# Recurrent mixer of a two-layer encoder: GpSimd's casts, splits, squares and sums placed on ScalarE and VectorE

## The chip, the core and the metric

One core of a Trainium2 chip runs the whole forward pass of a small encoder: TensorE (PE in the profile) for matrix products, VectorE (DVE), ScalarE (ACT), GpSimd (POOL) and SyncE (SP), which issues most loads. The metric is the device time of one execution in microseconds; lower is better.

## The reference

Two layers over 512 tokens of width 1024. Each layer is a mixer, a layer norm, a mixture of 16 experts and a second layer norm. The first layer mixes by attention, the second by a gated linear recurrence, and only that one is touched:

```python
def rg_lru(xc, w_a, b_a, w_x, b_x, lam, reverse):
    r = sigmoid(block_diag_linear(xc, w_a, b_a))
    i = sigmoid(block_diag_linear(xc, w_x, b_x))
    log_a = LRU_C * r * log_sigmoid(lam)
    a = exp(log_a)
    b = sqrt(-expm1(2.0 * log_a)) * (i * xc)
    _, h = associative_scan(combine, (a, b), reverse=reverse, axis=1)
    return h

def mixer_rglru(x, ...):
    gate, xr = split(x @ w_in, 2, axis=-1)
    xc = conv_b + sum(xp[:, k:k + seq] * conv_w[k] for k in range(4))
    h = rg_lru(xc, forward) + rg_lru(xc, backward)
    y = h * gelu(gate, approximate=True)
    return y @ w_out
```

All of it is in float32.

## The kernel before, in words

**Operands in two parts.** TensorE works here on rounded operands (type fp32r). Each float32 matrix is therefore split into a rounded part, the high half, and the rest, the low half, and a product is three matmuls: high by high, high by low and low by high. The split of a weight chunk of 128x1024 is two instructions in `plain`: a cast, which writes `wh`, and a subtraction, which writes `wl`. Nearly everywhere ScalarE casts (line 133) and VectorE subtracts (line 134). For the recurrent mixer two switches of `plain`, `hp` and `lp`, place the cast on GpSimd (line 131) and the subtraction on GpSimd as well. The string `CONV_X` says for each half chunk of the x projection which of these holds (b: cast on GpSimd; c: subtraction on GpSimd; so they alternate), and `MIXED2` says it for the gate projection: both casts, and the second subtraction.

**Loads.** `Stream` and `Items` hold the weights in the order of use. A chunk is 1 MB (or 512 KB of gate weights) and lands in one of two buffers (`raw`); its load is issued by SyncE when the chunk two before it has been split. `hl` has four pairs of high and low tiles. In the mixer the chunks come in this order: x0, x1, x2, w0, x3, w1, g0, w2, g1, w3, g2, g3; x and g are chunks of the two halves of the input projection (two half chunks each), w are gate weights. In the names of the trace half chunks 217 and 218 belong to x2, 219 to w0, 220 and 221 to x3, 222 to w1, 223 and 224 to g0, 225 to w2, 226 and 227 to g1, 228 to w3, 229 and 230 to g2, 231 and 232 to g3; from 233 on they are the output projection's.

**The mixer, `mixer1`.** The channels are worked on in four chunks of 256 (two blocks `f` of 128), with the 512 tokens along the free side. For each chunk: `proj("x")` fills two PSUM tiles; `conv` makes the convolution of four taps, one on ScalarE (line 1071) and three on VectorE (line 1074), and splits the result (lines 1077 and 1078); `gates` makes, for each block and both directions, two gate products (lines 1107 to 1109) into PSUM, two gate tanh (line 1113), the exponential `a` (line 1115), a further tanh (line 1116), the product `i` (line 1117), the square `u` of `a`, on GpSimd (line 1119), and the product of line 1122. `scan` takes the square root of `u` for the whole chunk (line 1126), multiplies (line 1129), makes four scans on VectorE, two directions by two blocks (line 1132), and adds both directions into `yall`, on GpSimd (line 1133). `gelu` works on the gate projection of the chunk: square (line 1085), a multiply and add of two constants (line 1086), the product with x (line 1087), tanh (line 1088), and two products (lines 1089 and 1091). `split` makes the two parts of `yall` (lines 1137 and 1138) for the output projection `out_proj` (lines 918 to 920), which uses the same four PSUM banks as the projections.

**What sets the order.** Each engine takes its instructions in one fixed order. A scheduler of the framework has arranged that order ahead of time from the program; the change thus moves more than the lines it names. Across engines, tiles are guarded by semaphores: a buffer is written again only when its readers are done. The loop of `mixer1` runs one stage late: while chunk c is projected, the gates and scans of the chunk two before it are worked on.

```python
        for k, c2 in (("x", 2), ("x", 3), ("g", 0), ("g", 1)):
            g = c2 - 2 if k == "x" else c2 + 2
            proj(k, c2, 0)
            gates(g, 0)
            proj(k, c2, 1)
            gates(g, 1)
            if k == "x":
                conv(c2)
            scan(g)
            if k == "g":
                gelu(c2)
```

ScalarE holds one table of functions at a time; where the next function isn't in it, an ACT_TABLE_LOAD stands in its order. In the mixer the square root needs a table other than exp and tanh.

Of the kernel before, what the change touches and what calls it, by code (L numbers as in the profile page):

```python
# [20 lines left out]
D = 1024  # L21
# [6 lines left out]
FC = DE // P  # L28
CAP = 96
OV = 13  # L30
CONV_X = "bcbcbcbc"
TAIL = ("a0 m0 a1 m1 v0 v1 h0 f0 h1 f1 a2 m2 a3 m3 v2 v3 h2 f2 h3 f3",
        "a0 m0 a1 m1 v0 a2 m2 v1 k0 f0 a3 m3 v2 h1 f1 v3 h2 f2 h3 f3")
FPOS = (0, 1, 2, 4, 5, 6, 7, 8, 10, 13)
# [67 lines left out]


def layout(I):
    """The inputs as the kernel loads them: slices, copies and permutations of what came in, and constants."""
    c = host_consts()
    a = {n: np.ascontiguousarray(I[n]) for n in _INS}
    rows = lambda x, n: np.broadcast_to(np.asarray(x).reshape(1, n), (P, n))
# [16 lines left out]
    return a  # L125


def plain(a, w, hp=False, lp=False):
    def conv(nc, r, h, l):
        if hp:  # L130
            nc.gpsimd.tensor_scalar(h[:, :w], r[:, a:a + w], 1.0, 1.0, op0=ALU.mult, op1=ALU.mult)
        else:
            nc.scalar.copy(h[:, :w], r[:, a:a + w])  # L133
        (nc.gpsimd if lp else nc.vector).tensor_tensor(l[:, :w], r[:, a:a + w], h[:, :w].bitcast(F32), op=ALU.subtract)  # L134
    return conv


PLAIN2 = (plain(0, HALF), plain(HALF, HALF))
MIXED2 = (plain(0, HALF, True), plain(HALF, HALF, True, True))


class Stream:
# [56 lines left out]
class K:  # L199
# [667 lines left out]
    def mix1_items(self, it):  # L867
        I, nc = self.I, self.nc

        self.first_ins = []  # L870

        def ld_in(c0):
            def load(t):
                ins = nc.sync.dma_start(t.rearrange("p (a b) -> p a b", a=KC),
                                        I["l1_w_in"][:, c0:c0 + 256].rearrange("(a p) b -> p a b", p=P)).ins
                if len(self.first_ins) < 2:
                    self.first_ins.append(ins)
            return load

        def ld_g(c):  # L880
            def load(t):
                nc.sync.dma_start(t[:, :HALF], I["gates"][c])
            return load

        mix = dict(a=(False, False), b=(True, False), c=(False, True), d=(True, True))
        x = lambda c: it.add(("x", c), ld_in(D + 256 * c),
                             tuple(plain(i * HALF, HALF, *mix[CONV_X[2 * c + i]]) for i in range(2)))
        g = lambda c: it.add(("g", c), ld_in(256 * c), MIXED2)
        w = lambda c: it.add(("w", c), ld_g(c), PLAIN2[:1])
        for f, c in ((x, 0), (x, 1), (x, 2), (w, 0), (x, 3), (w, 1), (g, 0), (w, 2), (g, 1), (w, 3), (g, 2), (g, 3)):  # L890
            f(c)
        self.out_items(it, 1)
# [159 lines left out]
    def mixer1(self, st, xH, xL):  # L1052
# [28 lines left out]
        def gelu(c2):  # L1081
            for f in range(2):
                x = B["g", c2][f]
                q = wp.tile([P, S], F32, name=f"ge{c2}{f}", tag="ge", bufs=2)
                A.activation(q, x, AF.Square)
                V.tensor_scalar(q, q, G1 * G2, G1, op0=ALU.mult, op1=ALU.add)
                V.tensor_tensor(q, q, x, op=ALU.mult)
                A.activation(q, q, AF.Tanh)
                V.scalar_tensor_tensor(q, q, 1.0, x, op0=ALU.add, op1=ALU.mult)  # L1089
                c = 2 * c2 + f  # L1090
                V.tensor_tensor(yall[:, c], q, yall[:, c], op=ALU.mult)

        def gates(c2, f):
# [22 lines left out]
                A.activation(r, r, AF.Tanh, bias=cm, scale=cm)  # L1116
                V.scalar_tensor_tensor(ii[:, k], ii[:, k], 1.0, xc[:, f], op0=ALU.add, op1=ALU.mult)
            sl = slice(2 * f, 2 * f + 2)
            nc.gpsimd.tensor_tensor(u[:, sl], a[:, sl], a[:, sl], op=ALU.mult)
            for d in range(2):  # L1120
                k = 2 * f + d
                V.scalar_tensor_tensor(u[:, k], u[:, k], 1.0, tr[d], op0=ALU.add, op1=ALU.mult)
# [1 line left out]
        def scan(c2):  # L1124
            a, ii, u = R[c2]
            A.activation(u, u, AF.Sqrt, scale=1.0 / 16.0)
            for f in range(2):
                sl = slice(2 * f, 2 * f + 2)
                V.tensor_tensor(ii[:, sl], ii[:, sl], u[:, sl], op=ALU.mult)
                for d, o in ((0, slice(None)), (1, slice(None, None, -1))):  # L1130
                    k = 2 * f + d
                    V.tensor_tensor_scan(u[:, k, o], a[:, k, o], ii[:, k, o], 0.0, op0=ALU.mult, op1=ALU.add)
                nc.gpsimd.tensor_tensor(yall[:, 2 * c2 + f], u[:, 2 * f], u[:, 2 * f + 1], op=ALU.add)

        def split(c2):
            for c in (2 * c2, 2 * c2 + 1):
# [584 lines left out]
```

## Time and profile before

| what | value |
|---|---|
| median of 3 runs | 1189.37 us (1189.37 to 1190.99) |
| profiled execution, first to last instruction (span) | 1188.6 us |
| that span beside the median | 0.8 us below it; a separate time of that execution is not listed |
| TensorE matmuls busy | 1056.6 us, 89% |
| VectorE busy | 953.0 us, 80% |
| ScalarE busy | 768.1 us, 65% |
| GpSimd busy | 318.2 us, 27% |
| mean granted TensorE clock | 0.937 |

Busy shares are means over stages that differ: the recurrent mixer takes some 180 of the 1188.6 us, from the end of the first layer at about 595 to the start of the output projection at about 763. What a stage is limited by is read from a window on it, and what an instruction costs from its own line or from the timeline. A mean above the shortest of the same shape says that some of a group's instructions took longer than their work.

### The profile page before, as it was taken

To read this page: it belongs to the slowest core of one execution; us is meant where nothing else is said; L and a number is where in the kernel's file an instruction comes from. 1 tells how busy PE (TensorE), PEld (TensorE's weight loads), DVE (VectorE), ACT (ScalarE), POOL (GpSimd) and SP (SyncE) were. 2 spreads that over 40 slices of the span, in tenths; PEclk is the share of its full clock that TensorE was granted. 3 is DMA by queue.
4 is the path that set the end of the run, shared out by engine and by line. 5 is a ranking of instruction groups with operands and counts; after the bars stand their busy time and mean duration, and the time that the engine had idled before them with its cause. 6 is when DMAs were issued, how large, how long until landed. Compare 5 with 4: busy or idle time off the path is not lost. (4 is left out here: it accounts for less than half of the span.)

```text
span 1188.6 us, 15070 instructions
## 1 busy us (share of the span) xinstructions
PE 1056.6 (89%) x5042; PEld 783.3 (66%) x5042; DVE 953.0 (80%) x1487; ACT 768.1 (65%) x1114; POOL 318.2 (27%) x278
## 2 busy tenths in 40 slices
PE   8999889986999999989789768797799999999892
PEld 6677677874777777756478546586577777776651
DVE  5685878367999999967767999947899998996785
ACT  5455778225788788757526665533578888876762
POOL 1112555125131121111234536203422211210122
PEclk9897999996999999989979969798799999999996
DMA  8180010877999999988713112295799999996983
GB/s 288 54 260 21 2 36 18 335 263 263 324 348 371 360 365 355 345 295 300 188 55 106 35 54 72 87 365 206 269 335 336 380 374 367 387 332 204 335 268 108
DMA packets 132693, 281.25 MB, mean 237 GB/s; under 512 B 8872, under 2 KB 32584, under 8 KB 132480
## 3 DMA queue, kind: packets, MB, share of 16 engines
q1 hardware_dynamic: 121344, 245.20, 56.8%
q0 software_dynamic: 10928, 33.93, 11.9%
q10 hardware_dynamic: 336, 1.08, 0.2%
q8 instruction: 42, 0.69, 0.2%
q14 instruction: 43, 0.35, 0.1%
HBM read 261.41 MB, written 23.74 MB: 240 GB/s over the span
## 5 line engine op out<-in xcount | busy, mean ns | idle before, releaser
L134 DVE TENSOR_TENSOR wl<-rr,wh 128x1024 fp32r<-128x1024 f32 x180 | 212.2, 1218 | 20.9 <-ACT wh L133 20.1
L133 ACT CAST wh<-rr 128x1024 fp32r<-128x1024 f32 x180 | 180.2, 1049 | 39.6 <-PE p L587 34.1
L134 DVE TENSOR_TENSOR wl<-rf,wh 128x1024 fp32r<-128x1024 f32 x104 | 123.8, 1219 | 17.5 <-ACT wh L133 17.3
L133 ACT CAST wh<-rf 128x1024 fp32r<-128x1024 f32 x104 | 105.2, 1048 | 43.4 <-PE p L587 15.1
L134 DVE TENSOR_TENSOR wl<-raw,wh 128x1024 fp32r<-128x1024 f32 (+1 forms) x97 | 116.1, 1225 | 20.2 <-ACT wh L133 11.6
L133 ACT CAST wh<-raw 128x1024 fp32r<-128x1024 f32 (+1 forms) x93 | 92.8, 1031 | 25.5 <-PE p L587 6.0
L636 POOL DMA_INDIRECT ybuf<-y,dst x30 | 57.2, 1907 | 185.7 <-ACT y L635 175.4
L625 PE MATMUL py<-wh,hh 128*96 128x512 f32 x256 | 102.9, 410 | 3.0 <-ACT y L635 1.8
L626 PE MATMUL py<-wl,hh 128*96 128x512 f32 x256 | 102.8, 402 | 1.6 <-DVE wl L134 1.6
L553 POOL DMA_INDIRECT xg<-hbuf,idx x32 | 41.0, 1280 | 236.1 <-PE xt L566 213.2
L583 PE MATMUL p<-wh,xh 128*96 128x512 f32 x256 | 102.8, 401 | 1.4 <-ACT xh L567 1.4
L627 PE MATMUL py<-wh,hl 128*96 128x512 f32 x256 | 102.6, 404 | 0.9 <-DVE hl L605 0.9
L586 PE MATMUL p<-wl,xh 128*96 128x512 f32 x256 | 101.4, 396 | 0.0
L584 PE MATMUL p<-wl,xh 128*96 128x512 f32 x256 | 101.4, 396 | 0.0
L585 PE MATMUL p<-wh,xh 128*96 128x512 f32 x256 | 101.1, 395 | 0.3
L588 PE MATMUL p<-wh,xl 128*96 128x512 f32 x256 | 101.1, 395 | 0.0
L587 PE MATMUL p<-wh,xl 128*96 128x512 f32 x256 | 100.7, 393 | 0.0
L134 DVE TENSOR_TENSOR wl<-rx,wh 128x1024 fp32r<-128x1024 f32 x56 | 66.1, 1219 | 7.6 <-ACT wh L133 7.6
L133 ACT CAST wh<-rx 128x1024 fp32r<-128x1024 f32 x56 | 56.2, 1050 | 9.9 <-PE p L587 7.6
L625 PEld LDWEIGHTS py<-wh,hh 128*96 128x96 f32 x256 | 42.1, 166 | 25.0 <-issue 4.9
L918 PE MATMUL pom<-wh,x 128*128 128x512 f32 x128 | 52.2, 408 | 4.4 <-DVE ge L1089 4.4
L627 PEld LDWEIGHTS py<-wh,hl 128*96 128x96 f32 x256 | 42.5, 166 | 19.8 <-DVE hl L605 1.8
(410 smaller groups left out, 2600.2 us busy)
## 6 DMA issues: line engine op xcount, KB each, us to landing
rr<-l_w SPq DMA_DIRECT2D x124, 512.0 KB, 11.2
rf<-l_w SPq DMA_DIRECT2D x68, 512.0 KB, 13.0
rr<-l_w SPq DMA_DIRECT2D x28, 1024.0 KB, 13.6
rx<-l_w SPq DMA_DIRECT2D x36, 512.0 KB, 10.6
raw<-l_w SPq DMA_DIRECT2D x36, 512.0 KB, 12.9
rf<-l_w SPq DMA_DIRECT2D x15, 1024.0 KB, 13.0
raw<-l_w SPq DMA_DIRECT2D x13, 1024.0 KB, 6.5
raw<-l_w_in SPq DMA_DIRECT2D x11, 1024.0 KB, 5.5
```

The source lines that it names most:

```text
L133: nc.scalar.copy(h[:, :w], r[:, a:a + w])
L134: (nc.gpsimd if lp else nc.vector).tensor_tensor(l[:, :w], r[:, a:a + w], h[:, :w].bitcast(F32), op=ALU.subtract)
L583: nc.tensor.matmul(p1, H[:, kc], w1h[:, sl], start=f, stop=False)
L584: nc.tensor.matmul(p1, H[:, kc], w1l[:, sl], start=False, stop=False)
L585: nc.tensor.matmul(p3, H[:, kc], w3h[:, sl], start=f, stop=False)
L586: nc.tensor.matmul(p3, H[:, kc], w3l[:, sl], start=False, stop=False)
L587: nc.tensor.matmul(p1, L[:, kc], w1h[:, sl], start=False, stop=e)
L588: self.last_mm = nc.tensor.matmul(p3, L[:, kc], w3h[:, sl], start=False, stop=e).ins
L625: nc.tensor.matmul(py[n], H[:, c], a, start=c == 0, stop=False)
L626: nc.tensor.matmul(py[n], H[:, c], b, start=False, stop=False)
L627: nc.tensor.matmul(py[n], L[:, c], a, start=False, stop=c == FC - 1)
L636: nc.gpsimd.indirect_dma_start(out=self.ybuf[l], out_offset=bass.IndirectOffsetOnAxis(ap=dst, axis=0), in_=y, in_offset=None, bounds_check ...
```

## The change

The weights of the mixer are split as everywhere else: cast on ScalarE, subtraction on VectorE. The square of `a` is a Square on ScalarE. The two sums into `yall` become one on VectorE over both blocks. In `gelu` the multiply and add and the product become one instruction, (q + 1/G2) times x, and the constants go into the scale of the tanh. Nothing else is changed; line numbers of the changed kernel are some 3 to 8 lower.

```diff
-CONV_X = "bcbcbcbc"
...
-def plain(a, w, hp=False, lp=False):
+def plain(a, w):
     def conv(nc, r, h, l):
-        if hp:
-            nc.gpsimd.tensor_scalar(h[:, :w], r[:, a:a + w], 1.0, 1.0, op0=ALU.mult, op1=ALU.mult)
-        else:
-            nc.scalar.copy(h[:, :w], r[:, a:a + w])
-        (nc.gpsimd if lp else nc.vector).tensor_tensor(l[:, :w], r[:, a:a + w], h[:, :w].bitcast(F32), op=ALU.subtract)
+        nc.scalar.copy(h[:, :w], r[:, a:a + w])
+        nc.vector.tensor_tensor(l[:, :w], r[:, a:a + w], h[:, :w].bitcast(F32), op=ALU.subtract)
     return conv
...
-MIXED2 = (plain(0, HALF, True), plain(HALF, HALF, True, True))
...
-        mix = dict(a=(False, False), b=(True, False), c=(False, True), d=(True, True))
-        x = lambda c: it.add(("x", c), ld_in(D + 256 * c),
-                             tuple(plain(i * HALF, HALF, *mix[CONV_X[2 * c + i]]) for i in range(2)))
-        g = lambda c: it.add(("g", c), ld_in(256 * c), MIXED2)
+        x = lambda c: it.add(("x", c), ld_in(D + 256 * c))
+        g = lambda c: it.add(("g", c), ld_in(256 * c))
...
                 A.activation(q, x, AF.Square)
-                V.tensor_scalar(q, q, G1 * G2, G1, op0=ALU.mult, op1=ALU.add)
-                V.tensor_tensor(q, q, x, op=ALU.mult)
-                A.activation(q, q, AF.Tanh)
+                V.scalar_tensor_tensor(q, q, 1.0 / G2, x, op0=ALU.add, op1=ALU.mult)
+                A.activation(q, q, AF.Tanh, scale=G1 * G2)
...
-            nc.gpsimd.tensor_tensor(u[:, sl], a[:, sl], a[:, sl], op=ALU.mult)
+            A.activation(u[:, sl], a[:, sl], AF.Square)
...
-                nc.gpsimd.tensor_tensor(yall[:, 2 * c2 + f], u[:, 2 * f], u[:, 2 * f + 1], op=ALU.add)
+            u4 = u.rearrange("p (f d) s -> p f d s", f=2)
+            V.tensor_tensor(yall[:, 2 * c2:2 * c2 + 2], u4[:, :, 0], u4[:, :, 1], op=ALU.add)
```

The order on ScalarE at the end of the gates of the first chunk, up to its square root (`u0` holds the squares, `a0` the exponentials, `xc2` the third chunk's convolution, `wh222` a weight's high half), before:

```order
L1116 ACTIVATE tr10_6651<-tr10_6651,cl_1194 128x512
L1113 ACTIVATE i0_6584<-pg13_6667,hb_1197 128x512
L1115 ACTIVATE a0_6583<-tr11_6665,cl_1194 128x512
L1071 ACTIVATE xc2_6678<-ppx20_6551,call_75 128x512
L1116 ACTIVATE tr11_6665<-tr11_6665,cl_1194 128x512
L1071 ACTIVATE xc2_6678<-ppx21_6552,call_75 128x512
L1126 ACT_TABLE_LOAD
L1126 ACTIVATE u0_6585<-u0_6585 128x2048
L1113 ACT_TABLE_LOAD
```

and of the change:

```order
L1107 ACTIVATE a0_6583<-tr11_6665,cl_1194 128x512
L129 CAST wh222_6707<-raw112_6705 128x1024
L1108 ACTIVATE tr11_6665<-tr11_6665,cl_1194 128x512
L1111 ACTIVATE u0_6585<-a0_6583 128x1024
L1064 ACTIVATE xc2_6678<-ppx20_6551,call_75 128x512
L1064 ACTIVATE xc2_6678<-ppx21_6552,call_75 128x512
L1105 ACTIVATE tr20_6742<-pg20_6738,hb_1197 128x512
L1118 ACT_TABLE_LOAD
L1118 ACTIVATE u0_6585<-u0_6585 128x2048
L1105 ACT_TABLE_LOAD
L1105 ACTIVATE i1_6736<-pg21_6744,hb_1197 128x512
```

The square of `a0` (line 1111) and the cast of `wh222` now stand between the last exponential and the root; the cast stood earlier before, and the square was not on this engine.

The order on VectorE behind the gates of the second chunk (`wl225` is the low half of the third chunk's gate weights; `i1` and `u1` belong to the second chunk; `xc3` is the last convolution), before:

```order
L1122 SCALAR_TENSOR_TENSOR u1_6738<-u1_6738,tr20_6743 128x512
L1122 SCALAR_TENSOR_TENSOR u1_6738<-u1_6738,tr21_6757 128x512
L1117 SCALAR_TENSOR_TENSOR i1_6737<-i1_6737,xc1_6538 128x512 x2
L134 TENSOR_TENSOR wl225_6862<-raw114_6859,wh225_6861 128x1024
L1122 SCALAR_TENSOR_TENSOR u1_6738<-u1_6738,tr30_6804 128x512
L1122 SCALAR_TENSOR_TENSOR u1_6738<-u1_6738,tr31_6818 128x512
L1074 SCALAR_TENSOR_TENSOR xc3_6831<-ppx30_6700,call_75,xc3_6831 128x510
```

and of the change:

```order
L1121 TENSOR_TENSOR i1_6736<-i1_6736,u1_6737 128x1024 x2
L1071 TENSOR_TENSOR xcL3_6840<-xc3_6830,xcH3_6839 128x1024
L1124 SCALAR_TENSOR_TENSOR u1_6737<-a1_6735,i1_6736 128x512 x4
L130 TENSOR_TENSOR wl225_6860<-raw114_6857,wh225_6859 128x1024
L1126 TENSOR_TENSOR yall_6302<-u1_6737 128x1024
L130 TENSOR_TENSOR wl226_6924<-raw115_6921,wh226_6923 128x1024
L1079 SCALAR_TENSOR_TENSOR ge00_6990<-ge00_6990,ppg00_6851 128x512
```

`wl225` stood ahead of the last convolution and of the second chunk's scans; it stands behind the four scans now, and the sum into `yall` (line 1126) and the low halves of the next gate projection follow it.

The order on VectorE from the last chunk's products and scans on (`u3`, `i3`; `wl231` and `wl232` are the low halves of the last gate projection's weights; `ge11` and `ge20` are gelu tiles), before:

```order
L1129 TENSOR_TENSOR i3_7044<-i3_7044,u3_7045 128x1024 x2
L1132 SCALAR_TENSOR_TENSOR u3_7045<-a3_7043,i3_7044 128x512 x4
L1086 TENSOR_SCALAR ge20_7225<-ge20_7225 128x512
L1086 TENSOR_SCALAR ge21_7232<-ge21_7232 128x512
L1087 TENSOR_TENSOR ge20_7225<-ge20_7225,ppg20_7161 128x512
L1087 TENSOR_TENSOR ge21_7232<-ge21_7232,ppg21_7162 128x512
L134 TENSOR_TENSOR wl233_7244<-raw119_7241,wh233_7243 128x1024
L134 TENSOR_TENSOR wl234_7272<-raw119_7241,wh234_7271 128x1024
```

and of the change:

```order
L1121 TENSOR_TENSOR i3_7039<-i3_7039,u3_7040 128x1024 x2
L1124 SCALAR_TENSOR_TENSOR u3_7040<-a3_7038,i3_7039 128x512 x4
L1081 SCALAR_TENSOR_TENSOR ge11_7147<-ge11_7147,ppg11_7003 128x512
L1126 TENSOR_TENSOR yall_6302<-u3_7040 128x1024
L1083 TENSOR_TENSOR yall_6302<-ge11_7147,yall_6302 128x512
L130 TENSOR_TENSOR wl231_7162<-raw118_7159,wh231_7161 128x1024
L130 TENSOR_TENSOR wl232_7190<-raw118_7159,wh232_7189 128x1024
L1079 SCALAR_TENSOR_TENSOR ge20_7217<-ge20_7217,ppg20_7153 128x512
L1079 SCALAR_TENSOR_TENSOR ge21_7223<-ge21_7223,ppg21_7154 128x512
L130 TENSOR_TENSOR wl233_7234<-raw119_7231,wh233_7233 128x1024
```

The low halves of the last projection's weights stand behind the last scans now; before, `wl231` stood further up, ahead of the last chunk's products, and `wl232` was GpSimd's.

## Rows read from the trace of the kernel before

**Rows 1.** Windows: busy us and instruction counts per engine, then clock, DMA share, GB/s.

```profile
760.00:770.00 10.00, 5.72 (x14) 4.11 (x15) 10.00 (x17) 6.22 (x10) 0.00 (x0) 0.66 0.42 152
...
624.90:775.85 150.95, 117.18 (x485) 92.21 (x484) 140.57 (x138) 94.00 (x124) 63.76 (x35) 0.89 0.22 73
```

**Rows 2.** VectorE's groups, 624.8 to 775.85: busy us, mean ns | idle before.

```profile
L1132 DVE TENSOR_TENSOR_SCAN u<-a,i 128x512 f32<-128x512 f32 x16 | 22.6, 1467 | 0.0
L1122 DVE SCALAR_TENSOR_TENSOR u<-u,tr 128x512 f32<-128x512 f32 x16 | 21.5, 1382 | 3.8 <-POOL u L1119 3.8
L1117 DVE SCALAR_TENSOR_TENSOR i<-i,xc 128x512 f32<-128x512 f32 x16 | 20.4, 1295 | 2.9 <-ACT i L1113 2.9
...
L1086 DVE TENSOR_SCALAR ge<-ge 128x512 f32<-128x512 f32 x8 | 7.8, 985 | 0.0
...
L1078 DVE TENSOR_TENSOR xcL<-xc,xcH 128x1024 fp32r<-128x1024 f32 x4 | 4.8, 1212 | 0.4 <-ACT xcH L1077 0.4
```

**Rows 3.** Single lines of VectorE: shortest, median and longest in ns.

```profile
L1117 DVE SCALAR_TENSOR_TENSOR i<-i,xc x16: 662/1459/2379, 640.2 to 741.4; 128x512 f32<-128x512 f32 x16
L1122 DVE SCALAR_TENSOR_TENSOR u<-u,tr x16: 677/690/2897, 647.8 to 743.2; 128x512 f32<-128x512 f32 x16
L1074 DVE SCALAR_TENSOR_TENSOR xc<-ppx,call,xc x24: 731/740/752, 627.2 to 687.5; 128x511 f32<-128x511 f32 x16, 128x510 f32<-128x510 f32 x8
```

**Rows 4.** Timeline of VectorE: start us, us, then line and operation.

```profile
652.72 2.38 DVE L1117 SCALAR_TENSOR_TENSOR i<-i,xc 128x512 f32<-128x512 f32 x1
```

**Rows 5.** Timeline of GpSimd at the same time.

```profile
652.07 2.48 POOL L1119 TENSOR_TENSOR u<-a 128x1024 f32<-128x1024 f32 x1 [0.95 <-ACT a L1115]
```

**Rows 6.** GpSimd's groups, 624 to 777.

```profile
L1119 POOL TENSOR_TENSOR u<-a 128x1024 f32<-128x1024 f32 x8 | 18.8, 2350 | 5.4 <-ACT a L1115 5.4
L134 POOL TENSOR_TENSOR wl<-raw,wh 128x1024 fp32r<-128x1024 f32 x6 | 16.0, 2667 | 5.3 <-ACT wh L133 5.0
L1133 POOL TENSOR_TENSOR yall<-u 128x512 f32<-128x512 f32 x8 | 14.2, 1773 | 45.6 <-DVE u L1132 45.6
L131 POOL TENSOR_SCALAR wh<-raw 128x1024 fp32r<-128x1024 f32 x10 | 13.2, 1328 | 28.4 <-PE ppx L1044 13.8 <-DVE ge L1089 7.2 <-DVE xcL L1078 5.7
```

**Rows 7.** Timeline of ScalarE: two casts, and four instructions in line.

```profile
591.54 1.97 ACT L133 CAST wh<-raw 128x1024 fp32r<-128x1024 f32 x2
...
697.84 0.68 ACT L1113 ACTIVATE i<-pg,hb 128x512 f32<-128x512 f32 x1
698.41 0.82 ACT L1115 ACTIVATE a<-tr,cl 128x512 f32<-128x512 f32 x1
699.11 0.59 ACT L1085 ACTIVATE ge<-ppg 128x512 f32<-128x512 f32 x1
699.59 0.82 ACT L1116 ACTIVATE tr<-tr,cl 128x512 f32<-128x512 f32 x1
```

**Rows 8.** Timeline of ScalarE: the four square roots, and a table load.

```profile
661.04 1.92 ACT L1126 ACTIVATE u<-u 128x2048 f32<-128x2048 f32 x1
...
684.69 1.28 ACT L1126 ACT_TABLE_LOAD   x1
685.99 1.91 ACT L1126 ACTIVATE u<-u 128x2048 f32<-128x2048 f32 x1
...
712.54 1.92 ACT L1126 ACTIVATE u<-u 128x2048 f32<-128x2048 f32 x1
...
745.23 1.91 ACT L1126 ACTIVATE u<-u 128x2048 f32<-128x2048 f32 x1
```

**Rows 9.** Timeline of TensorE: last gate projection, then output projection.

```profile
744.61 0.77 PE L1042 MATMUL ppg<-x,wh 128*128 128x512 f32 x1 [6.36 <-DVE ge L1089]
...
762.72 0.50 PE L918 MATMUL pom<-wh,x 128*128 128x512 f32 x1 [4.44 <-DVE ge L1089]
765.12 0.79 PE L920 MATMUL pom<-wh,x 128*128 128x512 f32 x1 [1.56 <-DVE x L1138]
```

**Rows 10.** DMA issues by line: count, KB, median us from issue to landing.

```profile
raw<-l_w_in SPq DMA_DIRECT2D x11, 1024.0 KB, 5.5
```

## The prediction

> **What bounds the kernel now.** I read the stretches first, then each engine's lines, then the timelines of the stretch that the change touches. The recurrent mixer's core lies at 624.9 to 775.85 us: there VectorE is busy for 140.57 of 150.95 us, TensorE for 117.18 at a mean granted clock of 0.89, ScalarE for 94.00 and GpSimd for 63.76, with the DMA engines at 0.22 [rows 1]. VectorE leaves 10.4 us unused, so it sets the pace, and TensorE is starved by it.
>
> A good part of VectorE's time is not work. The products of line 1117 and line 1122 take 1295 and 1382 ns in the mean [rows 2], but 662 and 677 ns at best and 2379 and 2897 at worst [rows 3]. Line 1074, of the same length but with one operand in PSUM, stays within 731 to 752 ns throughout [rows 3]. The timeline shows what the slow ones have in common: one product started at 652.72 and took 2.38 us, to 655.1 [rows 4]; GpSimd ran its square from 652.07 to 654.55 [rows 5]. So a VectorE instruction whose operands are all in SBUF stands still while GpSimd works there. The excess is 16 x (1.295 - 0.662) = 10.1 us and 16 x (1.382 - 0.677) = 11.3 us, 21.4 together; scans and other lines show some more, which I leave as margin.
>
> For the whole of the moved work the Trainium skill ("SBUF — State Buffer", "Who interferes with whom") gives more: the ports that VectorE and GpSimd share are an exclusive lock, held for a whole instruction, and the loser blocks fully. By that alone up to GpSimd's 18.8 + 16.0 + 14.2 + 13.2 = 62.2 us [rows 6] could come back; the rows show about a third, since GpSimd often runs when VectorE waits or reads PSUM. The measured 21.4 goes into the sum.
>
> **The change part by part.** *Off GpSimd:* 32 instructions of this stretch, 62.2 us [rows 6]. The excess of 21.4 goes with them, if nothing else takes their place; what stays on GpSimd here are two memsets and a few DMA issues.
>
> *Onto VectorE:* six low splits and four joined sums of 128x1024 elements. The split of line 1078 has the same shape, 4.8/4 = 1.2 us [rows 2], so 10 x 1.2 = 12.0. The sums read with a stride; twice a 128x512 product at its best (1.32) is the other bound, 1.2 more in all. *Off VectorE:* eight instructions of line 1086, 7.8 us with their own excess [rows 2]; the product that replaces line 1087 is of line 1117's kind and length and costs the same. VectorE alone: -21.4 + 12.0 - 7.8 = -17.2 us, if it waits no longer than now.
>
> *Onto ScalarE:* ten casts and eight squares of 128x1024 elements. Two casts take 1.97 us [rows 7], 0.98 each; the squares have the same length and count alike: 18 x 0.98 = 17.6 us on an engine with 57 us free in this stretch. So the ScalarE queue has to be followed. The points to follow it by are the four square roots, at 661.04, 685.99, 712.54 and 745.23 [rows 8]: 84.2 us from first to last. Prices in line come from successive starts: gate tanh 0.57, exp (and the second tanh, and the convolution's first term) 0.70, gelu square 0.48 [rows 7]; root 1.92, table load 1.28 [rows 8]. The order of the changed kernel has, from root to root:
> 1. first to second: root, two loads, 7 x 0.57, 10 x 0.70, six casts or squares: 1.9 + 2.6 + 4.0 + 7.0 + 5.9 = 21.4;
> 2. second to third: root, two loads, 10 x 0.57, 8 x 0.70, 2 x 0.48, six: 22.6;
> 3. third to fourth: root, two loads, 9 x 0.57, 8 x 0.70, 2 x 0.48, four: 20.1.
>
> In the second, the gate weights' low split (wl225) now stands behind the four scans on VectorE. Behind the root VectorE has two products, a split, four scans and wl225, eight steps of 1.2 = 9.6 us, while ScalarE runs dry after three casts, two squares and a load, 5.2: it stands 9.6 - 5.2 = 4.4 us, as the gates' matmuls need that split. So 64.1 + 4.4 = 68.5 in place of 84.2: **-15.7**. Ahead of the first root I take a quarter of the excess, 5.4, less a quarter of the added VectorE work, 3.0, plus 1.5 for a square on the chain that falls from 2.48 [rows 5] to 0.98: **-3.9**. Handovers between engines take an instruction's length rather than the spacing in line, about 0.1 (0.67 against 0.57), some 24 times: **+2.4**. The fourth root comes 17.2 earlier, at 728.0.
>
> The end is TensorE's. The last gate projection needs wl231, which VectorE reaches after two products, four scans, a short product, the sum and another short product: 1.9 + 10.8 behind the root's start, at 740.7 with wl231 itself. Its 48 matmuls took from 744.61 to 758.28, where the 4.44 of idleness begins [rows 9]; the same 13.7 brings them to 754.4. The output projection, which started at 762.72 [rows 9], can follow at once, as by then two PSUM pairs and the first splits are ready: -8.3. It also loses its wait of 1.56 at 765.12 [rows 9], and it no longer enters after 4.44 us of idleness: the granted clock was 0.66 at 760 to 770 [rows 1], partly 1.2 and partly 2.4 GHz, so 0.34 x 10 = 3.4. Sum: -8.3 - 1.6 - 3.4 = **-13.3 us**. From there TensorE's work and the weight loads follow as before: the loads wait for buffers that these same splits free, so they move along with them.
>
> The profiled span is 1188.6, the median 1189.37, 0.8 above it; 1188.6 - 13.3 + 0.8 = **1176.1 us**. Before 624.9 the moved casts and splits cost nothing that I count: two splits land in VectorE's wait for the last expert; if that cover failed they would cost 2.4, about what two collisions there give back.
>
> **Rivals.**
> *More comes back.* Scans and the layer norm ahead of this stretch lose collisions too, and TensorE stays at its high clock. VectorE without a wait would need 140.57 - 17.2 = 123.4 us of 150.95, so 27.6 is the most; three quarters of the 14.3 beyond my sum give 1165. For it: the scans' 1467 ns spread [rows 2] is not in my sum. Against: three engines now share the pace, and each wait counts.
>
> *Less: low splits late.* The stand of 4.4 recurs for the third chunk's gates and for the last projection, where splits too stand behind scans: 2 x 4.4 = 8.8, so 1184.9. For it: the order. Against: the casts there are ready early.
>
> *Slower: ScalarE held by loads.* Casts of the chunks from DMA now stand in ScalarE's queue ahead of gates; with two load buffers a chunk is only requested when VectorE has split the chunk two before it. A load takes 5.5 us to land [rows 10]. Held five times (two gate weights, three projections) for 4 us each: -13.3 + 20 = +6.7, so 1196. It decides from 13.3/5 = 2.7 us each. Against it: the DMA share of 0.22 [rows 1], and by my walk only one cast meets its load, within 1 us.
>
> *Slower: tables.* If a square needed another table than exp and tanh, each of the eight would bring two loads of 1.28: 20.5 us on ScalarE, 1176.1 + 20.5 = 1196.6. The rows speak against it: a square at 699.11 stands right between exp and tanh, with no load [rows 7]. The Trainium skill ("ScalarE: Activation LUTs", "Table sets: the hidden batching unit") names relu, copy, identity and abs as fillers of every set, and not the square. By that list the loads would come; by the trace they don't, and the trace decides.
>
> *The stretching has another cause,* and stays: then VectorE gains 12.0 and loses 7.8, +4.2, 1193.6. The pair of slow product and square speaks against it [rows 4, 5].
>
> **How the numbers follow.** Forecast 0.65 (its own range 1169 to 1183); more 0.13 (1165); less 0.10 (1184.9); loads 0.06; tables 0.01; other cause 0.02; no change in sum 0.03. About 0.2% (2.4 us) is what a measurement of this kernel can tell. Faster: 0.65 + 0.13 + 0.10 = 0.88; same 0.03; slower 0.09. The range, 1164 to 1186, leaves out the slower cases, no change, and part of the larger gain. The prices' bounds lie inside it: squares at a 128x1024 cast or 0.1 more (+0.8), the strided sums (+1.2).
>
> **What would show it.** Right: lines 1109 and 1114 of the changed kernel at a mean near 0.7 us; roots some 20 to 23 us apart; ScalarE near 110 us busy in the stretch, the same nine table loads; the last projection ending near 754. Wrong: VectorE products still over 1 us, ScalarE's casts waiting for loads, more table loads, or TensorE's waits for low splits above 20 us in sum.

## The result, and the profile after

The changed kernel takes **1174.55 us** in the median of four runs (1172.14 to 1176.07) against 1189.37 for the kernel before (four runs, 1184.59 to 1190.99); the ratio of the times, estimated from the single runs, is **0.9885, 95% interval [0.9855, 0.9916]**, and that of the two medians 0.9875. The forecast was 1176.1, faster. The profiled execution took 1172.14 us, its span is 1170.1.

That span is 18.5 us shorter than the one before, more than the change can claim. One event that the change does not touch shows it: GpSimd's scatter near the end of the first expert stage, the one after 18.1 us of idleness (timelines of GpSimd, before and after; start us, us, line, operation):

```profile
558.81 1.43 POOL L636 DMA_INDIRECT ybuf<-y,dst  x1 [18.12 <-ACT y L635]
```
```profile
554.65 1.43 POOL L631 DMA_INDIRECT ybuf<-y,dst  x1 [18.13 <-ACT y L630]
```

The after execution was 4.16 us ahead before anything had been moved. So from here on I count from this scatter (the expectations below call it the stage's last; one more follows). Between kernels that share all code ahead of it, it started anywhere from 554.4 to 559.3; but the stretch behind it repeats: one kernel, profiled on two occasions, reached the output projection at 186.72 and 186.75 us behind it.

The stretches of the changed kernel (busy us and counts by engine, then clock, DMA share, GB/s), to set beside [rows 1]:

```profile
624.90:757.60 132.70, 114.77 (x460) 88.64 (x459) 113.17 (x138) 108.70 (x139) 2.99 (x4) 0.91 0.25 83
...
744.00:764.00 20.00, 20.00 (x87) 16.08 (x86) 15.78 (x28) 9.25 (x13) 0.55 (x1) 1.00 0.57 200
```

VectorE, third in the row, is now idle for 132.70 - 113.17 = 19.5 us, where it left 10.4. The row before begins at the first low split of the stretch; that split starts at 622.13 here, and from there VectorE is busy for 114.80 of 135.47 us, idle for 20.7. ScalarE is at 108.70, GpSimd at 2.99. Around the output projection's start TensorE is busy throughout, with a granted clock of 1.00 in place of 0.66.

VectorE's groups of that stretch (busy us, mean ns), to set beside [rows 2]:

```profile
L130 DVE TENSOR_TENSOR wl<-raw,wh 128x1024 fp32r<-128x1024 f32 x19 | 23.1, 1219 | 1.3 <-ACT wh L129 1.3
L1124 DVE TENSOR_TENSOR_SCAN u<-a,i 128x512 f32<-128x512 f32 x16 | 18.4, 1206 | 0.0
...
L1109 DVE SCALAR_TENSOR_TENSOR i<-i,xc 128x512 f32<-128x512 f32 x16 | 10.8, 686 | 4.0 <-ACT i L1105 4.0
L1114 DVE SCALAR_TENSOR_TENSOR u<-u,tr 128x512 f32<-128x512 f32 x16 | 10.3, 688 | 5.7 <-ACT u L1111 5.7
```

And single lines (shortest, median, longest ns), to set beside [rows 3]:

```profile
L1109 DVE SCALAR_TENSOR_TENSOR i<-i,xc x16: 664/688/693, 637.5 to 718.6; 128x512 f32<-128x512 f32 x16
...
L1114 DVE SCALAR_TENSOR_TENSOR u<-u,tr x16: 682/688/693, 645.0 to 722.0; 128x512 f32<-128x512 f32 x16
```

The long tails are gone: 693 ns at worst, where it was 2379 and 2897. The scans, which I had left as margin, fell from 22.6 us to 18.4.

ScalarE's four square roots, to set beside [rows 8]:

```profile
655.17 1.92 ACT L1118 ACTIVATE u<-u 128x2048 f32<-128x2048 f32 x1
...
676.50 1.92 ACT L1118 ACTIVATE u<-u 128x2048 f32<-128x2048 f32 x1
...
704.50 1.92 ACT L1118 ACTIVATE u<-u 128x2048 f32<-128x2048 f32 x1
...
724.65 1.91 ACT L1118 ACTIVATE u<-u 128x2048 f32<-128x2048 f32 x1
```

They are 21.33, 28.00 and 20.15 us apart, 69.5 in all, where it was 84.2. TensorE's timeline shows the waits that remain, and the output projection's start (pom), to set beside [rows 9]:

```profile
688.14 2.07 PE L1101 MATMUL pg<-xcH,wl 128*128 128x512 f32 x4 [3.85 <-DVE wl L130]
...
734.08 0.50 PE L1035 MATMUL ppg<-x,wh 128*128 128x512 f32 x1 [2.96 <-DVE ge L1081]
...
736.95 1.22 PE L1037 MATMUL ppg<-x,wl 128*128 128x512 f32 x2 [2.13 <-DVE wl L130]
...
749.62 0.39 PE L911 MATMUL pom<-wh,x 128*128 128x512 f32 x1
```

The projection starts at 749.62 with no wait ahead of it; it was 762.72 after 4.44 us of idleness. Counted from the scatter that is 194.97 against 203.91.

One stretch got worse. ScalarE's timeline at the entry, then TensorE's:

```profile
584.62 1.04 ACT L129 CAST wh<-raw 128x1024 fp32r<-128x1024 f32 x1 [9.85 <-DMA raw<-l_w_in]
585.57 0.68 ACT L647 ACTIVATE yh<-py,gpos 96x512 fp32r<-96x512 f32 x1
...
586.30 0.79 PE L655 MATMUL pd<-yh,ot 96*128 96x512 f32 x1 [5.31 <-ACT yh L647]
```

The first chunk's cast stands 9.85 us for its load, with the activation of the last expert behind it in ScalarE's queue, and TensorE stands 5.31 us for that.

### The profile page after: what moved, and what is told of

Read it like the earlier page. It is cut to its first block, busy times and chain, and to the rows that moved or that the text cites. A ratio compares the mean times of both kernels' runs of the same rounds, so it can differ in the third digit from the quotient of the medians.

```text
span 1170.1 us, 15042 instructions
## 1 busy us (share of the span) xinstructions
PE 1050.8 (90%) x5042; PEld 777.5 (66%) x5042; DVE 925.9 (79%) x1491; ACT 786.9 (67%) x1134; POOL 248.2 (21%) x242
## 5 line engine op out<-in xcount | busy, mean ns | idle before, releaser
L130 DVE TENSOR_TENSOR wl<-rr,wh 128x1024 fp32r<-128x1024 f32 x180 | 212.3, 1220 | 22.2 <-ACT wh L129 21.6
L130 DVE TENSOR_TENSOR wl<-raw,wh 128x1024 fp32r<-128x1024 f32 (+1 forms) x105 | 125.2, 1218 | 29.0 <-ACT wh L129 28.7
L129 ACT CAST wh<-raw 128x1024 fp32r<-128x1024 f32 (+1 forms) x105 | 105.3, 1033 | 41.9 <-DMA raw<-l_w_in 15.1
L622 PE MATMUL py<-wh,hl 128*96 128x512 f32 x256 | 101.9, 401 | 0.9 <-DVE hl L600 0.9
L581 PE MATMUL p<-wl,xh 128*96 128x512 f32 x256 | 101.7, 397 | 0.0
L579 PE MATMUL p<-wl,xh 128*96 128x512 f32 x256 | 101.7, 397 | 0.0
L620 PEld LDWEIGHTS py<-wh,hh 128*96 128x96 f32 x256 | 41.7, 164 | 24.9 <-issue 4.9
L621 PEld LDWEIGHTS py<-wl,hh 128*96 128x96 f32 x256 | 42.2, 165 | 18.7 <-DVE wl L130 3.1
```

Of the source, the lines that this page charges most:

```text
L130: nc.vector.tensor_tensor(l[:, :w], r[:, a:a + w], h[:, :w].bitcast(F32), op=ALU.subtract)
L579: nc.tensor.matmul(p1, H[:, kc], w1l[:, sl], start=False, stop=False)
L581: nc.tensor.matmul(p3, H[:, kc], w3l[:, sl], start=False, stop=False)
L620: nc.tensor.matmul(py[n], H[:, c], a, start=c == 0, stop=False)
L621: nc.tensor.matmul(py[n], H[:, c], b, start=False, stop=False)
L622: nc.tensor.matmul(py[n], L[:, c], a, start=False, stop=c == FC - 1)
```

## The experiments

All kernels in one table: us from the scatter to the mixer's first transpose, to the first root, between roots, from the fourth root to the output projection with the gate branch's matmuls (ppg) in that time, and to the output projection in all. The last column is the timed ratio to the kernel before.

| kernel | transpose | root 1 | to 2, 3, 4 | root 4 to projection | projection | ratio, 95% |
|---|---|---|---|---|---|---|
| before | 36.2 | 102.2 | 24.95, 26.55, 32.69 | 17.5 (48) | 203.9 | 1 |
| changed | 43.2 | 100.5 | 21.33, 28.00, 20.15 | 25.0 (68) | 195.0 | 0.9885 [0.9855, 0.9916] |
| e1 casts back | 34.6 | 99.1 | 23.90, 23.06, 23.05 | 17.7 (43) | 186.7 | 0.9831 [0.9799, 0.9862] |
| e2 casts only | 42.2 | 99.4 | 24.47, 24.43, 27.55 | 20.5 (57) | 196.4 | 0.9915 [0.9886, 0.9945] |
| e3 first chunk back | 36.2 | 101.2 | 21.32, 27.47, 20.16 | 24.9 (68) | 195.0 | 0.9915 [0.9883, 0.9947] |
| e4 idle squares | 43.6 | 101.9 | 22.87, 29.97, 21.94 | 25.1 (71) | 201.8 | 0.9950 [0.9929, 0.9970] |
| e5 gate chunks back | 42.6 | 103.0 | 23.90, 19.47, 24.72 | 16.7 (44) | 187.7 | 0.9879 [0.9828, 0.9929] |
| e6 conv chunks back | 36.2 | 97.5 | 21.32, 28.18, 20.15 | 24.7 (68) | 191.8 | 0.9881 [0.9843, 0.9919] |
| e7 w2 earlier | 43.4 | 101.7 | 21.32, 22.77, 28.66 | 16.0 (50) | 190.5 | 0.9891 [0.9842, 0.9940] |
| e8 g3 earlier | 43.6 | 102.0 | 21.31, 28.18, 20.10 | 22.2 (67) | 193.8 | 0.9881 [0.9833, 0.9929] |
| e9 = e6 + e7 | 34.6 | 95.9 | 21.32, 22.64, 28.38 | 17.4 (49) | 185.6 | 0.9843 [0.9814, 0.9872] |
| e10 = e1 again | 34.6 | 99.0 | 23.91, 23.04, 23.05 | 17.7 (43) | 186.8 | 0.9828 [0.9800, 0.9856] |
| e11 idle memsets | 42.8 | 100.0 | 21.32, 28.51, 20.85 | 24.2 (68) | 194.9 | 0.9936 [0.9910, 0.9963] |
| e12 squares only | 36.2 | 102.2 | 24.90, 24.55, 24.75 | 18.0 (43) | 194.4 | 0.9886 [0.9854, 0.9918] |

The timed intervals of the changed kernel and of e3, e5, e6, e7, e8 and e12 all overlap. What is said below of differences among these is read from one profiled execution of each, from the scatter to the projection, and the times alone do not show it.

### Does GpSimd's work make VectorE stand? (e4, e11)

e4 adds to the changed kernel squares on GpSimd that nobody reads; e11 adds fills in their place.

```diff
 e4:      A.activation(u[:, sl], a[:, sl], AF.Square)
+         dj = wp.tile([P, S], F32, name=f"dj{c}", tag="dj", bufs=1)
+         for k in (2 * f, 2 * f + 1):
+             nc.gpsimd.tensor_tensor(dj, a[:, k], a[:, k], op=ALU.mult)
 e11:     V.scalar_tensor_tensor(u[:, k], u[:, k], 1.0, tr[d], op0=ALU.add, op1=ALU.mult)
+         nc.gpsimd.memset(tr[d], 0.0)
+         nc.gpsimd.memset(tr[d], 0.0)
```

> The changed kernel, and besides GpSimd squares each block of a into a scratch tile that nobody reads (two squares of 128x512 for each 128x1024 of ScalarE's, 16 in all, some 19 us of GpSimd). Nothing waits for them, so only contention can cost time. Theory A: the squares were 18.8 of 62.2 us of GpSimd's work, so 18.8/62.2 x 21.4 = 6.5 us of VectorE's time stretch again, in the products of a and u; the core is longer by 5 to 8 us: 1180 to 1183. Theory B (chains alone): within 1 us of the changed kernel, products at 0.69 us.

> The changed kernel, and behind each of VectorE's sixteen products of u GpSimd fills the tile that it has just read with zeros, twice (32 fills of 128x512, nobody reads them). GpSimd works on SBUF here without reading it, beside the same VectorE instructions as in the run with unread squares. If any work of GpSimd on SBUF makes VectorE stand: products and scans stretch per us of GpSimd as in that run (7.8 us of excess on 20.6 us of squares, 0.38 us for each), so about 6 us on 15 us of fills, 1178 to 1181. If only its reading, or its two-operand instructions, do so: products at 0.69 and scans at 1.21 us, within 1.5 us of the changed kernel.

Groups of e4 in its mixer (625 to 768), VectorE's and GpSimd's, and a pair from their timelines:

```profile
L130 DVE TENSOR_TENSOR wl<-raw,wh 128x1024 fp32r<-128x1024 f32 x20 | 25.7, 1289 | 7.8 <-ACT wh L129 7.8
L1127 DVE TENSOR_TENSOR_SCAN u<-a,i 128x512 f32<-128x512 f32 x16 | 21.6, 1407 | 0.0
L1109 DVE SCALAR_TENSOR_TENSOR i<-i,xc 128x512 f32<-128x512 f32 x16 | 12.4, 787 | 4.0 <-ACT i L1105 4.0
L1117 DVE SCALAR_TENSOR_TENSOR u<-u,tr 128x512 f32<-128x512 f32 x16 | 12.0, 789 | 2.9 <-ACT u L1111 2.9
...
L1114 POOL TENSOR_TENSOR dj<-a 128x512 f32<-128x512 f32 x16 | 20.6, 1286 | 95.2 <-ACT a L1107 95.2
...
675.53 1.50 POOL L1114 TENSOR_TENSOR dj<-a 128x512 f32<-128x512 f32 x1 [1.08 <-ACT a L1107]
676.06 2.12 DVE L1117 SCALAR_TENSOR_TENSOR u<-u,tr 128x512 f32<-128x512 f32 x2
```

Groups of e11 (620 to 765):

```profile
L1126 DVE TENSOR_TENSOR_SCAN u<-a,i 128x512 f32<-128x512 f32 x16 | 18.4, 1206 | 0.0
...
L1109 DVE SCALAR_TENSOR_TENSOR i<-i,xc 128x512 f32<-128x512 f32 x16 | 10.9, 686 | 5.3 <-ACT i L1105 5.3
L1114 DVE SCALAR_TENSOR_TENSOR u<-u,tr 128x512 f32<-128x512 f32 x16 | 10.3, 687 | 6.1 <-ACT u L1111 6.1
...
L1115 POOL MEMSET tr<- 128x512 f32 x16 | 8.4, 527 | 98.8 <-DVE u L1114 98.8
L1116 POOL MEMSET tr<- 128x512 f32 x16 | 8.4, 526 | 0.9
```

Squares that read SBUF stretch the scans by 0.20 us each, the products by 0.10 and the splits by 0.07: 3.2 + 1.6 + 1.6 + 1.4 = 7.8 us on 20.6 us of GpSimd's work. The pair shows one: two products in a row take 2.12 us, where the changed kernel's pairs take 1.29. The projection comes 6.8 us later. Nobody waits for these squares, so **the collision is shown**, and it costs nearly its full excess. The fills, 16.8 us on the same SBUF and behind the same products, stretch no product and no split beside them (686, 687 ns), and the projection stays at 194.9. By the start and end of every instruction, 7.9 us of fills lay beside products and 1.2 beside splits; none lay beside a scan, so the scans' 1206 ns say nothing of fills. So it is GpSimd's reading that collides. That it needn't read two operands is seen in e1, described below: six scans there lay beside GpSimd's casts alone, which read one operand, and two of these took 1.99 and 2.00 us, the others 1.19 to 1.21 as undisturbed ones do. The Trainium skill ("SBUF — State Buffer", "Who interferes with whom") says the same: a VectorE instruction with two SBUF inputs contends with a GpSimd instruction that reads SBUF, not with one that only writes it. By these two runs, the trace agrees.

e11's median, 1177.95 us, lies above what I expected for that case, though its mixer lost nothing. The runs do not tell where the difference lies; its interval just touches the changed kernel's and overlaps e4's. By their times alone e4 and e11 can't be told apart: it is the trace that does it. e4's median, 1178.62 us, is a little under the 1180 to 1183 expected.

### Which part brought the gain? (e12, e2, e1)

e12 is the kernel before with the squares on ScalarE, e2 the kernel before with the casts and splits moved, e1 (and e10) the changed kernel without the moved casts and splits. The lines shown leave out the switches of `plain`, `CONV_X`, `mix` and `MIXED2`, which come and go with them.

```diff
 e12:
-            nc.gpsimd.tensor_tensor(u[:, sl], a[:, sl], a[:, sl], op=ALU.mult)
+            A.activation(u[:, sl], a[:, sl], AF.Square)
 e1, against the changed kernel (e2 is the reverse, against the kernel before):
-        x = lambda c: it.add(("x", c), ld_in(D + 256 * c))
-        g = lambda c: it.add(("g", c), ld_in(256 * c))
+        x = lambda c: it.add(("x", c), ld_in(D + 256 * c),
+                             tuple(plain(i * HALF, HALF, *mix[CONV_X[2 * c + i]]) for i in range(2)))
+        g = lambda c: it.add(("g", c), ld_in(256 * c), MIXED2)
```

> The kernel before with only the squares moved to ScalarE; casts, splits, sums and the gelu as before. Of VectorE's excess 18.8/62.2 x 21.4 = 6.5 us belong to the squares, and each square is 1.4 us shorter on the chain to the root, four of them on the path at most: the output projection 6.5 to 12 us earlier than before against the first stage's last scatter (203.9), so 192 to 197; time 1175 to 1183. If the sums and the gelu's shorter chain carry the gain of the version with all casts back (186.7), it stays above 198.

> The kernel before with only the weight casts and low splits moved off GpSimd. Theory A: 10.0 us of VectorE's excess go, 7.2 us of splits come, so the core gains about 3 us, and the entry's stand costs 5 to 7: 1189.4 - 3 + 6, so 1190 to 1195. Theory B: VectorE sets the pace and gets 7.2 us more, and the entry's stand: 1189.4 + 7 + 6 = 1202. If the entry's stand is made up for later: 1186.

> The changed kernel with the weight casts and low splits back on GpSimd as before; squares, joined sums and the gelu's constant stay as changed. Theory A (VectorE's instructions stand while GpSimd works on SBUF): casts and splits were 29.2 of GpSimd's 62.2 us in the mixer's core, so 29.2/62.2 x 21.4 = 10.0 us of VectorE's excess come back, and six splits of 1.2 = 7.2 us leave VectorE; the core is longer by some 3 us. The entry's stand goes (ScalarE's cast that waits 9.85 us for its load ahead of an activation that the last expert needs; some 5 to 7 us in the changed kernel). Sum: 1174.6 + 3 - 6, so 1170 to 1173; lines 1109 and 1114's successors at a mean near 0.95 us, the first transpose of the mixer at the last expert's end as before. Theory B (the gain came from shorter chains alone: a square of 0.98 in place of 2.48, one gelu instruction fewer; GpSimd's neighbours cost VectorE nothing): the products stay at 0.69 us, and VectorE is relieved of 7.2 us of splits, so 1174.6 - 7 - 6 = 1162. If the casts were most of the gain: over 1180.

> The fastest version so far again, all casts and low splits back on GpSimd, on the same chip as the joined edits: 1162 to 1168, ratio to the kernel before 0.980 to 0.986; output projection within 0.7 us of 186.7 behind the first stage's last scatter. If the first result was the chip's, the ratio is near 0.988.

From the scatter to the projection: squares alone 203.9 to 194.4, casts and splits alone to 196.4, squares with sums and gelu to 186.7, all together to 195.0. **The parts do not add.** On the kernel before, the moved casts and splits gain 7.6 us, where I had expected a loss in either theory (its time is 1176.79; theory A had 1190 to 1195, and the case with the stand made up for 1186); on top of the other edits they lose 8.3. e1 beats both kernels, 1165.01 and again 1164.82 us, with intervals that barely touch the changed kernel's; there the sums and the gelu are worth 194.4 - 186.7 = 7.7 us beyond the squares. e12's 9.6 us lie inside the 6.5 to 12 expected; its time, 1173.06, came out under the 1175 to 1183.

e1's groups on VectorE (620 to 755):

```profile
L1116 DVE SCALAR_TENSOR_TENSOR i<-i,xc 128x512 f32<-128x512 f32 x16 | 15.6, 992 | 4.8 <-ACT i L1112 4.8
L1121 DVE SCALAR_TENSOR_TENSOR u<-u,tr 128x512 f32<-128x512 f32 x16 | 15.5, 1011 | 1.8 <-ACT u L1118 1.8
```

The collisions with GpSimd's casts and splits are back: 16 x (0.992 + 1.011 - 2 x 0.688) = 10.0 us, as expected, and still the projection comes 8.3 us earlier, and the time is 5 us under theory A's 1170 to 1173. So the excess is real, and something else is worth more.

### What costs the 8.3? (e5, e6, e3)

e5 gives back to GpSimd the gate branch's chunks alone, e6 the convolution branch's alone, e3 the first chunk alone.

```diff
 e5:
-        g = lambda c: it.add(("g", c), ld_in(256 * c))
+        g = lambda c: it.add(("g", c), ld_in(256 * c), MIXED2)
 e6: the two lines of x, as in e1
 e3:
+        early = (plain(0, HALF, True), plain(HALF, HALF, False, True))
-        x = lambda c: it.add(("x", c), ld_in(D + 256 * c))
+        x = lambda c: it.add(("x", c), ld_in(D + 256 * c), early if c == 0 else PLAIN2)
```

> The changed kernel with only the gate branch's four chunks (line 882's g) cast and split on GpSimd as before; the convolution branch's chunks stay as changed. With all chunks back the time was 1165.0 us, 10 below the changed kernel on the same chip. Theory C (place, not engine time: in the changed kernel the gate chunks' low splits stand on VectorE behind the scans, so that the third gate chunk is multiplied only after all matmuls of the last block's gates, and 68 matmuls of the gate branch are left at the fourth square root in place of 48): these chunks carry it all, 1164 to 1168, about 43 matmuls left at the fourth root. Theory D (time on engines: what VectorE and ScalarE are relieved of counts in proportion): half of it, since half of the chunks go back, so 1169 to 1171.

> The changed kernel with only the convolution branch's four chunks cast and split as before; the gate branch's stay as changed. TensorE's order of the gate matmuls and the place of the gate chunks' splits stay those of the changed kernel. Theory C: no gain, as for the first chunk alone: 1173 to 1177. Theory D: half of 10: 1169 to 1171.

> The changed kernel with the first weight chunk of the mixer alone treated as before: its first half cast on GpSimd, its second half split on GpSimd, all else as changed. If the cast that waits on ScalarE for its load (9.85 us, and TensorE 5.31 us behind it) is what the entry costs, TensorE's wait for ScalarE at the last expert goes and the mixer begins 5 us earlier against the expert stage: 1174.6 - 5 = 1169.5 (1167 to 1171). Rival: the mixer's first block is paced by VectorE and by the loads whatever the last expert does, and the stand is made up for: within 1.5 us of the changed kernel.

The gate branch's chunks carry 7.3 of the 8.3 us, with 44 matmuls left at the fourth root; the timed ratio alone, 0.9879, does not show it. The count is read in the windows from the fourth root to the output projection, of the tile ppg alone (first number TensorE's busy time). Changed kernel:

```profile
724.65:749.62 24.97, 18.82 (x68) 14.28 (x68) 3.31 (x5) 1.68 (x3) 0.86 0.41 146
```

e1:

```profile
725.32:742.97 17.65, 12.62 (x43) 9.55 (x41) 3.19 (x5) 1.75 (x3) 0.81 0.26 85
```

And a wait of TensorE's ahead of the fourth root, in the changed kernel:

```profile
716.81 0.74 PE L1037 MATMUL ppg<-x,wl 128*128 128x512 f32 x2 [2.36 <-DVE wl L130]
```

The fourth root starts at nearly the same time, but in the changed kernel 25 more of the gate branch's matmuls are still to be done, 18.82 - 12.62 = 6.2 us. In its program the third gate chunk is multiplied behind all of the last block's gate matmuls; in e1 ten matmuls of it stand among them. So moving a split did more than load VectorE: it changed the order in which TensorE's program was built. That order is ten of the 25. The other 15 are done in e1 between the last gate matmul and the root: 43 there in 12.8 us at a granted clock of 1.00, in the changed kernel 28 in 11.4 us at 0.85, with the wait of 2.36 us for a low split among them. How much of this follows from the order and how much from the split's lateness is not shown.

Theory D, half for half of the chunks, falls with that. Against theory C, though, the convolution chunks are not free either: e6 is 3.1 us earlier at the first root, and stays so. Its time, 1169.77, is what theory D gave and not theory C's 1173 to 1177, and the two parts together, 7.3 + 3.1, are more than the 8.3 of both at once: these parts don't add either. And e3 gives the entry's 7.0 us back at the first transpose (36.2), but the first root comes no earlier than in the changed kernel. e3's timelines show why:

```profile
603.66 2.34 POOL L133 TENSOR_TENSOR wl<-raw,wh 128x1024 fp32r<-128x1024 f32 x1
...
603.72 3.36 DVE L796 SCALAR_TENSOR_TENSOR xr<-xr,lw,b 128x1024 f32<-128x1024 f32 x1 [0.44 <-POOL lw L336]
...
608.28 0.80 PE L1041 MATMUL ppx<-x,wl 128*128 128x256 f32 x2 [3.78 <-DVE wl L133]
```

GpSimd's one split falls on the layer norm's product, which takes 3.36 us, where the same line takes 1.28 with GpSimd idle, and TensorE then stands 3.78 us for the low split behind it. The kernel before has this collision too (3.40 us), so that is part of what was won; the rest isn't followed up.

### Moving nothing but the place (e7, e8, e9)

Each is the changed kernel with one conversion asked for earlier, ahead of a block's scans; e9 has e6's edit too.

```diff
+EARLY = {("x", 3): ("w", 2)}        e7, e9
+EARLY = {("g", 1): ("g", 3)}        e8
+            if (k, c2) in EARLY:
+                st.conv_to(st.where[EARLY[k, c2]] + 1)
             scan(g)
```

> The changed kernel with nothing moved between engines: only the conversion of the third block's gate weights (wl225) is asked for before the second block's scans rather than behind them. On VectorE it then stands before half of those scans, and the third gate chunk's matmuls (229) lie among the last block's gate matmuls rather than behind them all. The prediction put the stand behind the second square root at 4.4 us, and the changed kernel shows TensorE waiting 3.85 us for this split. If the place of the splits costs what theory C says: the second to third root 24 us apart or less in place of 28.0, 1167 to 1171. If VectorE's four scans merely are late by what the split takes, or the matmuls that come earlier push others back: within 1.5 us of the changed kernel, so 1173 to 1176.

> The changed kernel with only the conversion of the last gate chunk's first half (wl231) asked for before the last block's scans: it then stands ahead of them on VectorE. TensorE's order does not change. In the changed kernel the last projection waits 2.13 us for this split, and starts at 735.67. Prediction's step (the last projection's start hangs on wl231): 2 us less, 1171 to 1174. Rival: behind it TensorE waits for the gelu of the second gate chunk, whose PSUM the last projection needs, and which VectorE reaches only after the scans and now 1.2 us later: 1175 to 1177.

> The changed kernel with the two edits joined that each gained between the first stage's last scatter and the first matmul of the mixer's output projection: the convolution branch's chunks back on GpSimd (195.0 to 191.8 us there, through the first root) and the third block's gate weights asked for before the second block's scans (195.0 to 190.5, through the second to third root). If they add: the output projection 195.0 - 3.2 - 4.5 = 187.3 us behind the scatter, the time 7.7 below the changed kernel's 1174.6, so 1165 to 1169. If they share one slack: 190, and 1169 to 1172.

e7 moves one weight chunk's split (wl225) ahead of the second block's scans, and no work between engines. Half of the scans were expected behind it; in the trace it starts at 683.19, and all four follow, from 687.73 on. Roots two and three come to stand 22.77 us apart in place of 28.00, three and four 28.66 in place of 20.15, 50 matmuls are left at the fourth root, and the projection comes 4.5 us earlier. The timed ratio, 0.9891 against 0.9885, does not show that. e8 gains 1.2 us, below the 2 expected: its wait for the split goes, but TensorE's wait for the second chunk's gelu grows from 2.96 to 5.2 us, as the rival had it. e9's two gains add (3.1 + 4.5 of 9.3 us, the rest at the first root), and it reaches the projection earliest of all, at 185.6; its time, 1168.07, is not distinguishable from e10's 1164.82. From the projection's start to the end e9's span is 3.5 us longer than e10's (422.4 against 418.9). In its first 20 us e9 does 82 matmuls and e10 88, with a wait of 1.05 us for a split of `yall` in e9, at 0.23 us each some 1.4 us; the rest no run here explains.

## Why the prediction was right, point by point

**VectorE's excess.** Right in cause and size: the two product lines lost 21.5 + 20.4 - 10.3 - 10.8 = 20.8 us, forecast 21.4 (e4 shows the cause, e12 and e1 the shares: 16 x (1.295 + 1.382 - 1.221 - 1.084) = 6.0 us for the squares, forecast 6.5 in e12's expectation). e12's means are in these groups (620 to 765):

```profile
L1117 DVE SCALAR_TENSOR_TENSOR i<-i,xc 128x512 f32<-128x512 f32 x16 | 19.2, 1221 | 4.8 <-ACT i L1113 4.8
L1122 DVE SCALAR_TENSOR_TENSOR u<-u,tr 128x512 f32<-128x512 f32 x16 | 16.7, 1084 | 1.8 <-ACT u L1119 1.8
```

The prediction's view that only about a third of GpSimd's 62.2 us is lost does not hold, nor does the reason that it gives. In the trace of the kernel before some 10 us of them ran while VectorE waited or read PSUM; 52 lay beside VectorE instructions with all operands in SBUF, and these took 34.8 us longer than their lines took alone. So VectorE's busy time fell by 140.57 - 114.80 = 25.8 us, from the first low split on, and not by 17.2. The surplus did not come out in the time: VectorE waits longer.

**What the sum hid.** By the prediction's own terms the moved casts and splits are a small gain: 29.2 of the 62.2 us, so 10.0 us of collisions, less 7.2 for six splits. At the output projection squares, sums and gelu alone gain 17.2 us (e1), and the casts and splits on top lose 8.3, more by where they stand than by what they load (e5, e7). The sum counted VectorE's time and did not price what the new order does to TensorE; a larger gain and an uncounted loss left 8.9 where 8.3 was forecast. That these cancel so nearly is luck.

**ScalarE's queue.** 21.4, 27.0 and 20.1 us between the roots were forecast, 21.33, 28.00 and 20.15 came. The stand for wl225 is there (3.85 us, forecast 4.4); e7 confirms that its place makes it. The 2.4 us added for handovers were too much: from first to last root 84.2 - 69.5 = 14.7 us were gained, where 15.7 - 2.4 = 13.3 was forecast.

**First root.** Forecast 3.9 us earlier, measured 1.7 against the scatter. The step that failed is "Before 624.9 the moved casts and splits cost nothing that I count". I looked at VectorE's wait alone and not at ScalarE's queue, where the first cast stands for its load ahead of the last expert: the rival of loads, priced at 4 us five times, came once at 9.85 us, in a place where I had not looked, and once at 0.81, in the mixer. The first put the first transpose 7.1 us back. Most of that was made up by the first root, and e3, which takes the stand away, gains nothing, so the stand is not shown to be what the first root lost. e6 shows 3.1 us to be had there from the convolution branch's casts and splits as a whole.

**Fourth root and end.** The fourth root: forecast 17.2 us earlier, measured 16.4; the first root's shortfall of 2.2 and the 1.4 too much for handovers nearly cancel, which is luck as well. Output projection: 8.3 and 8.9. Behind it, the lost wait and the clock: forecast 1.6 + 3.4 = 5.0; the span from the projection's start to the end went from 1188.6 - 762.72 = 425.9 to 1170.1 - 749.62 = 420.5, so 5.4. Its first 20 us hold 88 matmuls where they held 68, at a granted clock of 1.00 in place of 0.83: 20 more of 0.23 us each, an estimate of 4.6 us. The rest is within what this last part differs by among the changed kernel and e1 to e12, 418.7 to 422.4. Sum from the scatter: forecast -13.3, measured -8.9 - 5.4 = **-14.3**; the median moved by 14.8.

**The rivals.** Nine table loads as before, no VectorE products above 0.7 us, and TensorE's waits for low splits come to 12.8 us in the stretch. "More comes back" did not come in the changed kernel although VectorE has the time for it: 19.5 us idle. That a better order brings it, e1 and e9 show.

## What to carry to other kernels

Work beside VectorE on GpSimd has a price in VectorE's rows, and the spread of one line's durations (shortest against longest) gives it; look there before counting busy time. But price each moved instruction by its place in the new queue as well: who stands behind it, what it waits for, and whether the other engines' order changes with it. Here one weight chunk's split asked for earlier was worth 4.5 us, and leaving casts and splits where they were was worth 8.3, although that kept 10.0 us of collisions. And measure from an unmoved event to an unmoved event: the stretch of the one kernel that was profiled twice repeated to 0.1 us here, while single runs of one kernel lay 2 to 9 us apart.

## What the runs showed of the hardware

I had taken any work of GpSimd on SBUF to stop VectorE. The runs draw the line at reading: 20.6 us of squares cost VectorE 7.8 us; 16.8 us of fills, 9.1 of them beside products and splits, cost it nothing. In e4 VectorE lost 7.8 / 20.6 = 0.38 us for each us of GpSimd's work; in the change, products and scans together gave back (20.8 + 4.2) / 62.2 = 0.40. Instructions with one operand in PSUM were not affected: in the kernel before 4.5 us of GpSimd's casts and splits lay beside eight of the convolution's, and none took over 0.752 us, with or without. And two operands in SBUF are not needed to be stretched: line 1086 of the kernel before, which reads one, took 0.42 us alone and 1.93 in the mean of the three that lay beside GpSimd's squares and sums.
